# Feed-forward input products as seven block products of 320 columns instead of eight, with x parked in DRAM

## The chip, the cores and the metric

The kernel runs on one core of one Trainium2 chip. The metric is the device time of one execution in microseconds (us), the median of several runs. Engines are named as in the profile: PE (TensorE matmul), PEld (its weight load), DVE (VectorE), ACT (ScalarE), POOL (GpSimd), SP (the queue that issues most DMAs). PSUM is the memory that PE writes, SBUF the one that the other engines and the DMAs work in.

## The reference, cut to what matters

Two layers; in each a feed-forward half, a mixer and another feed-forward half. The change touches the feed-forward halves, which are this, on 640 tokens (512 latent, 128 context), D_MODEL = 1024 and D_FF = 2816:

```python
def swiglu(h, w_in, w_out):
    gate, up = jnp.split(h @ w_in, 2, axis=-1)
    return (jax.nn.silu(gate) * up) @ w_out

def adaln_sublayer(x, mod, s, g_pre, g_post, fn, weight):
    shift = mod[:, 3 * s, None]
    scale = mod[:, 3 * s + 1, None]
    gate = mod[:, 3 * s + 2, None]
    h = rmsnorm(x, g_pre) * (1 + scale) + shift
    y, aux = fn(h)
    return x + weight * gate * rmsnorm(y, g_post), aux
```

`mod` is SiLU(cond) @ mod_w[l] + mod_b[l], for two conditions (latent and context): 9 rows of 1024 per layer.

## The kernel before

**Arithmetic.** Every fp32 operand of a product is split into a rounded part `hi` and a rest `lo` (both fp32r), and a product is three passes: hi\*hi, hi\*lo, lo\*hi (`PASSES`). The split of a weight tile costs one ACT copy (line 102) and one DVE subtraction (line 103), of 128x1024 each.

**A feed-forward half (`ffn`).** The normed input lies transposed in `hT` (8 blocks of 128 features by 640 tokens, hi and lo). The 22 blocks of 128 hidden features, called f here, are worked in parts of 2, 4, 4, 4, 4, 4 (`PARTS`). For each f, `col_product` (line 467) forms the gate and the up product: 2 (gate, up) x 2 token groups (384 and 256 columns) x 8 feature blocks x 3 passes = 96 matmuls. `glu` (lines 512 and 513) makes silu(gate)\*up, and `split` (274, 275) gives `g`. After a part's f, `product` (line 573) multiplies `g` by the output weights, 120 matmuls of 512 columns for four f, and DVE adds the result to `yacc` (line 595). In the last part, tile after tile of 128 tokens is finished by `tail`: `emit` (products and the add of line 630), `post_norm` (399, 402), `pre_norm` (407), and `to_feature` (transposes 415, 418, 275) for the next sub-layer, in the order `TAIL_FFN`, where `m0` puts the products of the last f that were held back (`rest(1)`) between two tiles.

**Weights (`Stream`).** Tiles of 512 KB come in by SP (line 74) into three raw buffers, are split, and wait in five buffers of `whi` and `wlo` until `done`.

**Modulation rows (`mod_gen`).** Beside a feed-forward half DVE works out rows of `mod` for later sub-layers (lines 308 and 310: multiply-adds of 128x512), one unit at each `tick`. Of the 16 rows, the first half (called A; from 70 to 522 us) makes 7, the second (B; 901 to 1380 us) 3, the third (C; 1380 to 1864 us) 6, and the last (D; from 2204 us) none. Each half row ends in four small matmuls (line 332).

**Order.** Each engine runs its instructions in the order of its own queue; the framework fixes these orders when it builds the program. POOL has little to do here: the product with the gate in `post_norm` (399), small powers (391), and in A a chain of DMAs of its own for the bias tables (lines 1478 to 1490).

Of the kernel before, what the change touches and what calls it, by code (L numbers as in the profile page):

```python
# [44 lines left out]
TAIL_FFN = "e0 e1 p0 p1 e2 t0 p2 m0 e3 t1 p3 t2 e4 p4"  # L45
TAIL_MIX = "e0 e1 p0 p1 e2 t0 p2 e3 t1 p3 t2 e4 p4"
# [6 lines left out]


class Stream:
# [31 lines left out]
    def pump(self):
        while self.n_dma < min(len(self.specs), self.n_split + RAW_BUFS):
            self.load()
        while self._room():  # L90
            self.split()
            self.load()

    def split(self):
# [1824 lines left out]
```

## Time and profile before

| | us |
|---|---|
| median of 3 runs (2679.11 to 2680.49) | 2680.42 |
| the profiled execution: its own time | 2679.11 |
| the profiled execution: span from first to last instruction | 2677.3 |
| PE busy in that span | 2617.9 (98%) |
| DVE busy | 1535.6 (57%) |
| ACT busy | 929.4 (35%) |
| POOL busy | 218.9 (8%) |
| mean granted clock of TensorE | 0.995 of full speed |

The profiled execution took 1.8 us more than its span, and is 1.3 us below the median of the runs. The shares are means over stages: DVE's lies between 32% and 79% in single parts of the feed-forward halves. Busy time of PE counts matmuls whose ends are modelled; how fast it works is read from the time between the starts of matmuls of one kind.

### The profile page before, as it was taken

The numbers are of one execution on the slowest core, as the hardware profiler recorded it, in microseconds if no ns is written. First come the engines' busy times: TensorE is split into PE (matmuls) and PEld (weight loads), VectorE is DVE, ScalarE is ACT, GpSimd is POOL, SyncE is SP. The second block draws the span as 40 slices with busy tenths as digits, with TensorE's granted clock in tenths as the row PEclk, the third lists the DMA queues.
The fourth block names the chain that finished last, engine by engine and source line by source line (L and its number), as shares of the span: only waits on it lengthen the run. The fifth ranks groups of instructions, "written<-read, shape, count | busy, mean of one in ns | idle before, by whom it ended". The sixth has DMA issues, their size and how long they took to land.

```text
span 2677.3 us, 39659 instructions
## 1 busy us (share of the span) xinstructions
PE 2617.9 (98%) x16050; PEld 2353.1 (88%) x16050; DVE 1535.6 (57%) x2627; ACT 929.4 (35%) x1751; POOL 218.9 (8%) x284
## 2 busy tenths in 40 slices
PE   7999999999989999999999999999999999999998
PEld 6988999888766899999989889998999879999998
DVE  5877673655675755443377666535777764333334
ACT  4312222453465522222253222225555654222122
POOL 0000200301010000000020000003423200000001
PEclk9999999999989999999999999999999999999999
DMA  9665652222102444332236545322222223222221
GB/s 264 207 173 164 198 162 79 62 57 67 43 25 56 143 123 121 111 84 78 79 106 190 150 146 151 110 82 60 62 68 68 68 88 102 71 79 71 79 72 55
DMA packets 359719, 279.51 MB, mean 104 GB/s; under 512 B 43744, under 2 KB 296560, under 8 KB 359536
## 3 DMA queue, kind: packets, MB, share of 16 engines
q1 hardware_dynamic: 357232, 271.74, 35.0%
q0 software_dynamic: 1584, 3.93, 0.5%
q8 instruction: 126, 2.06, 0.3%
q10 hardware_dynamic: 720, 1.31, 0.1%
q14 instruction: 57, 0.47, 0.1%
HBM read 272.74 MB, written 8.11 MB: 105 GB/s over the span
## 4 chain that ended last, share of the span: by engine, by line
PE 61%; DVE 3%; DMA 2%; POOL 1%; issue 1%; ACT 1%; SPq 0%; DVEq 0%; POOLq 0%; ACTq 0%
PE ps L467 33%; PE ps L573 15%; PE ps L477 5%; PE ps L768 3%; DMA mraw<-in_mod_w_dram 1%; PE ps L1714 1%; PE ps L1695 1%; POOL tok L399 1%; PE sc L768 1%; PE ps L1665 1%; PE ps L1666 0%; DVE wlo L103 0%; DVE yacc L630 0%; DVE x L402 0%; PE ps L332 0%
## 5 line engine op out<-in xcount | busy, mean ns | idle before, releaser
L467 PE MATMUL ps<-hT,whi 128*128 128x384 f32 (+1 forms) x5760 | 1256.1, 309 | 6.7 <-DVE hT L275 3.6
L467 PEld LDWEIGHTS ps<-hT,whi 128*128 128x128 f32 x5760 | 968.1, 189 | 21.6 <-issue 7.8
L467 PE MATMUL ps<-hT,wlo 128*128 128x256 f32 (+1 forms) x2880 | 888.1, 308 | 0.0
L102 ACT CAST whi<-raw 128x1024 fp32r<-128x1024 f32 x312 | 327.4, 1051 | 968.6 <-PE ps L467 588.4
L103 DVE TENSOR_TENSOR wlo<-raw,whi 128x1024 fp32r<-128x1024 f32 x312 | 382.4, 1228 | 440.0 <-ACT whi L102 436.0
L467 PEld LDWEIGHTS ps<-hT,wlo 128*128 128x128 f32 x2880 | 545.5, 189 | 0.0
L573 PE MATMUL ps<-whi,g 128*128 128x512 f32 x1600 | 511.3, 395 | 4.2 <-ACT g L274 3.7
L573 PEld LDWEIGHTS ps<-whi,g 128*128 128x128 f32 x1600 | 300.3, 188 | 81.1 <-ACT g L274 5.0
L310 DVE SCALAR_TENSOR_TENSOR macc<-mraw,cc,macc 128x512 f32<-128x512 f32 x448 | 309.1, 747 | 34.7 <-DMA mraw<-in_mod_w_dram 34.5
L573 PE MATMUL ps<-wlo,g 128*128 128x512 f32 x800 | 317.5, 397 | 0.0
L477 PE MATMUL ps<-hT,whi 128*128 128x384 f32 (+1 forms) x1216 | 278.1, 316 | 0.0
L477 PEld LDWEIGHTS ps<-hT,whi 128*128 128x128 f32 x1216 | 204.1, 188 | 22.1 <-issue 15.3
L477 PE MATMUL ps<-hT,wlo 128*128 128x384 f32 (+1 forms) x608 | 188.9, 311 | 0.0
L573 PEld LDWEIGHTS ps<-wlo,g 128*128 128x128 f32 x800 | 150.2, 188 | 34.4
L399 POOL TENSOR_TENSOR tok<-yacc,G 128x1024 f32<-128x1024 f32 (+1 forms) x20 | 43.4, 2171 | 1538.2 <-DVE yacc L630 1535.5
L513 DVE TENSOR_TENSOR sg<-sg,ps 128x256 f32<-128x256 f32 (+1 forms) x176 | 85.1, 484 | 135.2 <-PE ps L467 129.3
L595 DVE TENSOR_TENSOR yacc<-yacc,ps 128x512 f32<-128x512 f32 x160 | 106.8, 685 | 89.7 <-PE ps L573 89.1
L512 ACT ACTIVATE sg<-ps 128x256 f32<-128x256 f32 (+1 forms) x176 | 76.3, 434 | 152.8 <-PE ps L467 101.2
L274 ACT CAST g<-sg 128x640 fp32r<-128x640 f32 (+2 forms) x96 | 65.6, 683 | 154.7 <-DVE sg L513 154.7
L477 PEld LDWEIGHTS ps<-hT,wlo 128*128 128x128 f32 x608 | 114.5, 188 | 1.1 <-issue 0.8
L275 DVE TENSOR_TENSOR g<-sg,g 128x640 fp32r<-128x640 f32 (+2 forms) x96 | 73.7, 768 | 52.5 <-ACT g L274 52.5
L1535 POOL TENSOR_TENSOR xn<-braw,mask 128x128 f32<-128x128 f32 x112 | 63.6, 597 | 136.0 <-DVE nb L1680 131.7
(358 smaller groups left out, 2374.4 us busy)
## 6 DMA issues: line engine op xcount, KB each, us to landing
raw<-in_ffn_w_in_dram SPq DMA_DIRECT2D x172, 512.0 KB
mraw<-in_mod_w_dram SPq DMA_DIRECT2D x128, 512.0 KB
raw<-in_ffn_w_out_dram SPq DMA_DIRECT2D x88, 512.0 KB
raw<-in_na_w_qkv_dram SPq DMA_DIRECT2D x24, 512.0 KB
raw<-in_ab_w_in_dram SPq DMA_DIRECT2D x22, 512.0 KB
raw<-in_mod_w_dram SPq DMA_DIRECT2D x32, 256.0 KB
G<-mod SPq DMA_DIRECT2D x12, 512.0 KB
mrow<-in_mod_b_dram SPq DMA_DIRECT2D x128, 32.0 KB
```

The costliest lines, as they stand in the source:

```text
L102: self.nc.scalar.copy(hi[:, :k * n], raw[:, :k * n])
L103: self.nc.vector.tensor_tensor(out=lo[:, :k * n], in0=raw[:, :k * n], in1=hi[:, :k * n].bitcast(F32), op=ALU.subtract)
L275: return a, nc.vector.tensor_tensor(out=lo, in0=src, in1=hi.bitcast(F32), op=ALU.subtract)
L310: nc.vector.scalar_tensor_tensor(out=acc[c], in0=raw[:, k2, :], scalar=w, in1=acc[c], op0=ALU.mult, op1=ALU.add)
L399: eng.tensor_tensor(out=yg[:, c0:c0 + n], in0=src, in1=G[cond_of(t)][:, c0:c0 + n], op=ALU.mult)
L467: nc.tensor.matmul(out=banks[grp], lhsT=w[a][:, k, :], rhs=hT[b][:, k, o:o + n], start=(k == 0 and (a, b) == (0, 0)), stop=(k == NK - 1 an ...
L477: nc.tensor.matmul(out=banks[grp], lhsT=w[a][:, k, :], rhs=hT[b][:, k, o:o + n], start=(k == 0 and (a, b) == (0, 0)), stop=(k == NK - 1 an ...
L512: nc.scalar.activation(out=sg[:, o:o + n], in_=banks[0][grp], func=AF.Silu)
L513: nc.vector.tensor_tensor(out=sg[:, o:o + n], in0=sg[:, o:o + n], in1=banks[1][grp], op=ALU.mult)
L573: nc.tensor.matmul(out=out, lhsT=g[a][kf][:, t * 128:(t + 1) * 128], rhs=w[b], start=(kf == 0 and (a, b) == (0, 0)), stop=(kf == len(fts) ...
L595: nc.vector.tensor_tensor(out=dst, in0=dst, in1=acc[t], op=ALU.add)
L768: nc.tensor.matmul(out=y[t][h], lhsT=hT[a][:, k, t * 128:(t + 1) * 128], rhs=ws[k // 2, h][b][:, k % 2, :], start=(k == 0 and (a, b) == (0 ...
```

## The change

Parts 1 to 5 of each feed-forward half (20 of 22 f, 80 in all) form [gate | up] by Strassen's scheme in Winograd's form. The block matrix of the weights has 2 x 2 blocks (feature halves by gate and up), that of the tokens too (feature halves by token halves of 320). Seven products `p1` to `p7` of 4 feature blocks x 3 passes = 12 matmuls of 320 columns each replace the 96 matmuls, so 84 for an f.

- **Weights.** A pair of raw tiles (gate G, up U) becomes four split tiles X, S, Z, V (S of half size). `_combine` makes their sums with four POOL operations of 128x512, in place in the raw buffers, once X has been split.
- **Tokens.** `combine` makes four sums of halves of `hT`, once in each half, in part 0 (two whole sums on POOL, two on DVE, four differences and four splits).
- **Results.** For each f ACT copies three results out of PSUM, DVE adds or multiplies four more from PSUM, and one more DVE product follows.
- **Space.** The sums of tokens take the room of x: x is written to DRAM by ACT's queue as it is made (`x_saved`) and read back by SP in the last part. `yacc` takes the x buffers.
- **Other.** `mod_gen` works in units of 256 KB (two DVE operations) instead of 512 KB (four); a tick between output products counts three times (`OUT_SHARE`); `load_gate` moves from part 2 to the last; `m0` falls away, instead the first output products of tile 0 run before the last two block products (`fill`); the loads of the first modulation rows come in pieces of 256 columns instead of 128; small tiles are padded to multiples of 64 bytes.

```diff
+    def _combine(self):
+        if not self.n_split:
+            return
+        _, _, kind, (g, *u) = self.specs[self.n_split - 1]
+        if kind != "X" or g in self.parts or u[0] not in self.raws:
+            return
+        G, U, S = self.raws[g], self.raws[u[0]], self.part_tile()
+        a, b = slice(0, 512), slice(512, 1024)
+        for out, in0, in1, op in (
+            (G[:, a], G[:, a], U[:, a], ALU.subtract), (S, U[:, b], G[:, a], ALU.subtract),
+            (U[:, a], U[:, a], U[:, b], ALU.add), (G[:, b], G[:, b], S, ALU.subtract),
+        ):
+            self.nc.gpsimd.tensor_tensor(out=out, in0=in0, in1=in1, op=op)
+        self.parts[g] = (S, self.n_pump)
...
+            def product(self, out, w, b, start):
+                for k in range(4):
+                    for a, c in PASSES:
+                        nc.tensor.matmul(
+                            out=out, lhsT=w[a][:, k, :], rhs=b[c][:, k, :], start=start and (k, a, c) == (0, 0, 0),
+                            stop=(k == 3 and (a, c) == PASSES[-1]), skip_group_check=not start,
+                        )
...
+            def p1(self):
...
+                self.X, self.Y = self.get("X"), bank([128, HALF])
+                self.product(self.Y, self.half(self.X, 0), B[0, 0], True)
+                nc.scalar.copy(self.t[:, 0], self.Y)
...
+            def p2(self):
+                W, t = bank([128, HALF]), self.t
+                self.product(W, self.half(self.X, 1), B[1, 0], True)
+                nc.vector.tensor_tensor(out=t[:, 0], in0=t[:, 0], in1=W, op=ALU.add)
+                nc.scalar.activation(out=t[:, 0], in_=t[:, 0], func=AF.Silu)
+                self.done("X")
...
+            def p6(self):
+                self.product(self.Y, self.get("S"), C[2], False)
+                nc.scalar.copy(self.t[:, 1], self.Y)
+                self.done("S")
...
+            def p5(self):
+                self.wz, self.Z = self.get("Z"), bank([128, HALF])
+                self.product(self.Z, self.half(self.wz, 0), C[1], True)
...
+            def p7(self):
+                self.V, t = self.get("V"), self.t
+                self.product(self.Y, self.half(self.V, 0), C[3], False)
+                nc.scalar.copy(t[:, 2], self.Y)
+                nc.vector.tensor_tensor(out=t[:, 2], in0=t[:, 2], in1=self.Z, op=ALU.add)
...
+            def p4(self):
+                t = self.t
+                self.product(self.Y, self.half(self.wz, 1), C[4], False)
+                nc.vector.tensor_tensor(out=t[:, 0], in0=t[:, 0], in1=self.Y, op=ALU.mult)
...
+            def p3(self):
+                t = self.t
+                self.product(self.Z, self.half(self.V, 1), B[1, 1], False)
+                nc.vector.tensor_tensor(out=t[:, 1], in0=t[:, 1], in1=self.Z, op=ALU.add)
+                nc.scalar.activation(out=t[:, 1], in_=t[:, 1], func=AF.Silu)
+                nc.vector.tensor_tensor(out=t[:, 1], in0=t[:, 1], in1=t[:, 2], op=ALU.mult)
+                self.out(1 if self.last else 0, 2)
+                self.done("V")
...
+            us = [Unit(f, g, i, f == fts[-1]) for i, f in enumerate(fts)]
+            for i, u in enumerate(us):
+                todo = [] if i else [u.p1]
+                todo += [u.p2] + ([us[i - 1].p3] if i else []) + [u.p6, u.p5, u.p7]
+                todo += [us[i + 1].p1, u.p4] if i + 1 < len(us) else [fill, u.p4, u.p3]
...
-        N, NQ = 512, 4
+        N, NQ = 512, NK
...
-TAIL_FFN = "e0 e1 p0 p1 e2 t0 p2 m0 e3 t1 p3 t2 e4 p4"
+TAIL = "e0 e1 p0 p1 e2 t0 p2 e3 t1 p3 t2 e4 p4"
```

How instructions move on DVE, in the units of a part of half A. `raw` and `whi`, `wlo` are weights and their parts, `sg` and `g` the hidden features before, `xn`, `tok` (f by turns) and `g` those now, `G` the tile of S, `macc` and `mraw` the modulation rows. Before, one f and the beginning of the next:

```order
L513 TENSOR_TENSOR sg<-sg,ps 128x384
L310 SCALAR_TENSOR_TENSOR macc<-mraw,cc,macc 128x512 x4
L103 TENSOR_TENSOR wlo<-raw,whi 128x1024
L513 TENSOR_TENSOR sg<-sg,ps 128x256
L310 SCALAR_TENSOR_TENSOR macc<-mraw,cc,macc 128x512 x2
L275 TENSOR_TENSOR g_1_1655<-sg,g_1_1651 128x640
L310 SCALAR_TENSOR_TENSOR macc<-mraw,cc,macc 128x512 x5
L103 TENSOR_TENSOR wlo<-raw,whi 128x1024
```

And now, the same place:

```order
L671 TENSOR_TENSOR xn<-xn,ps 128x320
L384 SCALAR_TENSOR_TENSOR macc<-mraw,cc,macc 128x512
L157 TENSOR_TENSOR wlo<-raw,whi 128x1024
L701 TENSOR_TENSOR tok<-tok,ps 128x320
L384 SCALAR_TENSOR_TENSOR macc<-mraw,cc,macc 128x512
L703 TENSOR_TENSOR tok<-tok 128x320
L384 SCALAR_TENSOR_TENSOR macc<-mraw,cc,macc 128x512
L157 TENSOR_TENSOR wlo<-G_2042,whi 128x512
L350 TENSOR_TENSOR g_1_1755<-tok,g_1_1751 128x640
L157 TENSOR_TENSOR wlo<-raw,whi 128x1024
L384 SCALAR_TENSOR_TENSOR macc<-mraw,cc,macc 128x512
L688 TENSOR_TENSOR xn<-xn,ps 128x320
```

An f had two weight splits, two products with PSUM and one split of `g` on DVE; it has four weight splits (one of half size), four operations with PSUM, one product in SBUF and the split of `g`, with the multiply-adds of the modulation rows between them.

On POOL, in half A around the DMAs of the bias tables (lines 1478 to 1490 before, 1689 to 1701 now). Before:

```order
L391 TENSOR_TENSOR r<-r,nhalf 128x1 x5
L1478 DMA rpb_flat<-tok 16x1x2
L1479 DMA rpb_flat<-tok 16x1x2
L1485 DMA rpb_rows<-rpb_flat 240x48 x16
L1490 DMA rel<-rpb_rows 16x16x384 x8
L399 TENSOR_TENSOR tok<-yacc_716,G_2218 128x1024
```

And now:

```order
L142 TENSOR_TENSOR raw<-raw,G_2868 128x512
L1689 DMA rpb_flat<-tok 16x1x2
L1690 DMA rpb_flat<-tok 16x1x2
L1696 DMA rpb_rows<-rpb_flat 240x48 x16
L1701 DMA rel<-rpb_rows 16x16x384
L142 TENSOR_TENSOR raw<-raw 128x512
L1701 DMA rel<-rpb_rows 16x16x384
L142 TENSOR_TENSOR G_3153<-raw 128x512
```

POOL, idle in the parts before, now makes four sums for each f, and one f's sums stand behind the waits of the bias tables' DMAs.

## Rows read from the trace of the kernel before

**Rows 1.** The page: busy time by engine, and the chain that ended last.

```profile
PE 2617.9 (98%) x16050; PEld 2353.1 (88%) x16050; DVE 1535.6 (57%) x2627; ACT 929.4 (35%) x1751; POOL 218.9 (8%) x284
PE 61%; DVE 3%; DMA 2%; POOL 1%; issue 1%; ACT 1%; SPq 0%; DVEq 0%; POOLq 0%; ACTq 0%
```

**Rows 2.** Busy time by stretch: parts 1 and 4 of A, one of B, C, D.

```profile
core 0: us, PE busy (x) PEld busy (x) DVE busy (x) ACT busy (x) POOL busy (x), PEclk, DMA share, GB/s
84.00:171.00 87.00, 87.00 (x535) 79.34 (x536) 68.84 (x101) 19.41 (x27) 0.00 (x0) 1.00 0.61 183
...
345.00:431.00 86.00, 86.00 (x533) 78.75 (x526) 50.20 (x75) 18.37 (x24) 0.00 (x0) 1.00 0.44 124
947.80:1032.70 84.90, 84.90 (x513) 78.89 (x512) 37.25 (x50) 19.21 (x26) 0.00 (x0) 1.00 0.35 102
1428.00:1514.00 86.00, 86.00 (x526) 79.15 (x520) 59.37 (x87) 18.78 (x25) 0.00 (x0) 1.00 0.55 158
2248.50:2332.70 84.20, 84.20 (x505) 78.74 (x504) 27.09 (x33) 19.21 (x26) 0.00 (x0) 1.00 0.23 69
```

**Rows 3.** The same view, line 467 alone, in a part's input products of D.

```profile
2248.50:2304.70 56.20, 56.18 (x384) 56.17 (x383) 1.00 0.25 76
```

**Rows 4.** Timeline of PE in D (start, us, engine, line): matmuls of 384 and 256 columns.

```profile
2249.05 0.51 PE L467 MATMUL ps<-hT,whi 128*128 128x384 f32 x2
...
2249.57 0.51 PE L467 MATMUL ps<-hT,whi 128*128 128x384 f32 x2
...
2253.04 0.40 PE L467 MATMUL ps<-hT,whi 128*128 128x256 f32 x2
...
2253.40 0.40 PE L467 MATMUL ps<-hT,whi 128*128 128x256 f32 x2
```

**Rows 5.** DVE's groups by form (count, busy us, mean ns, idle before and its releaser).

```profile
L103 DVE TENSOR_TENSOR wlo<-raw,whi 128x1024 fp32r<-128x1024 f32 x312 | 382.4, 1228 | 440.0 <-ACT whi L102 436.0 <-ACT wlo L906 1.2 <-issue 0.7
L310 DVE SCALAR_TENSOR_TENSOR macc<-mraw,cc,macc 128x512 f32<-128x512 f32 x448 | 309.1, 747 | 34.7 <-DMA mraw<-in_mod_w_dram 34.5
L595 DVE TENSOR_TENSOR yacc<-yacc,ps 128x512 f32<-128x512 f32 x160 | 106.8, 685 | 89.7 <-PE ps L573 89.1
L275 DVE TENSOR_TENSOR g<-sg,g 128x640 fp32r<-128x640 f32 x80 | 65.9, 823 | 44.1 <-ACT g L274 44.1
L513 DVE TENSOR_TENSOR sg<-sg,ps 128x384 f32<-128x384 f32 x88 | 48.7, 553 | 130.9 <-PE ps L467 129.3 <-ACT sg L512 1.5
L513 DVE TENSOR_TENSOR sg<-sg,ps 128x256 f32<-128x256 f32 x88 | 36.5, 414 | 4.4 <-ACT sg L512 4.4
L308 DVE TENSOR_SCALAR macc<-mraw,cc 128x512 f32<-128x512 f32 x64 | 29.8, 480 | 3.8 <-DMA mraw<-in_mod_w_dram 3.6
```

**Rows 6.** POOL's groups by form.

```profile
L399 POOL TENSOR_TENSOR tok<-yacc,G 128x1024 f32<-128x1024 f32 x15 | 37.0, 2463 | 1093.6 <-DVE yacc L630 1093.6
L1423 POOL TENSOR_TENSOR wlo<-ident,sums 128x512 f32<-128x512 f32 x8 | 8.3, 1040 | 70.5 <-DVE sums L1421 36.0 <-ACT hT L274 15.0 <-DVE nb L1337 13.8
L399 POOL TENSOR_TENSOR tok<-yacc,G 128x512 f32<-128x512 f32 x5 | 6.5, 1294 | 444.6 <-DVE yacc L630 441.9 <-DMA out_dram<-x 2.7
```

**Rows 7.** Timeline of DVE and POOL after half A: two splits beside POOL.

```profile
523.09 3.50 DVE L275 TENSOR_TENSOR hT<-xn,hT 128x512 fp32r<-128x512 f32 x2
523.32 2.72 POOL L399 TENSOR_TENSOR tok<-yacc,G 128x1024 f32<-128x1024 f32 x1 [2.13 <-DVE yacc L630]
```

**Rows 8.** Timelines of PE and of DVE in the tail of half A.

```profile
499.96 1.09 PE L415 MATMUL ps<-ident,xn 128*128 128x128 f32 x8 [0.71 <-DVE xn L407]
...
506.60 1.29 DVE L275 TENSOR_TENSOR hT<-xn,hT 128x512 fp32r<-128x512 f32 x2
...
510.60 0.75 DVE L407 TENSOR_SCALAR xn<-x,r 128x1024 f32<-128x1024 f32 x1 [0.44 <-POOL r L391]
```

**Rows 9.** Timeline of POOL in half A: the first and the last of the bias DMAs.

```profile
280.61 0.54 POOL L1478 DMA_DIRECT2D rpb_flat<-tok  x1 [256.27 <-DVE tok L1475]
...
299.02 4.48 POOL L1490 DMA_DIRECT2D rel<-rpb_rows  x8 [3.19 <-DMA rpb_rows<-rpb_flat]
```

More of the change, by code (lines that the diff above doesn't have):

```diff
@@ L74, in load, with _loads @@
             self.nc.sync.dma_start(out=view[p0:p0 + np_, :, c0:c0 + src.shape[-1]], in_=src)
-        self.raws.append(raw)
+        self.raws[self.n_dma] = raw
         self.n_dma += 1
+    def _loads(self):
+        while self.n_dma < len(self.loads) and self.n_dma - self.freed < RAW_BUFS:
+            self.load()
     def _room(self):
@@ L99, in split @@
         else:
+            self.held.add(key)
             hi = self.w_pool.tile([128, 1024], F32R, tag="whi", name="whi", bufs=W_BUFS)
@@ L113, in get, with done @@
         self.n_get += 1
+        self.got.append(key)
         return self.ready.pop(0)
-    def done(self, n=1):
-        self.n_done += n
+    def done(self, n=1, key=None):
+        for _ in range(n):
+            k = self.got.pop(0 if key is None else self.got.index(key))
+            self.held.discard(k)
         self.pump()
@@ L429, in to_feature, with tail @@
         return ins
-    def tail(emit, pieces, G, nxt, m, mid=None, between=None):
+    def tail(emit, pieces, G, nxt, m, junk, dst=None, between=None):
         xn = {}
@@ L436, in step @@
             emit(t)
-            post_norm(t, pieces(t), G, last=nxt is None)
+            post_norm(t, pieces(t), G, junk, dst and dst[t], last=nxt is None)
         def pre(t):
@@ new lines, in products @@
+                def products():
+                    for h in range(2):
+                        ws = [stream.get(("out", l, j, f, h)) for f in fts[::2]]
+                        for tiles in ((0, 1, 2), (3, 4)):
+                            acc = {t: bank() for t in tiles}
+                            for kf in range(len(fts)):
+                                for t in tiles:
+                                    product(acc[t], t, kf, [w[:, kf % 2, :] for w in ws[kf // 2]])
+                                if tiles[-1] == NT - 1 and kf % 2 == 1:
+                                    stream.done()
+                                if kf < len(fts) - 1:
+                                    yield
+                            for t in tiles:
+                                dst = yacc[t][:, h * 512:(h + 1) * 512]
+                                if p == 0:
+                                    nc.scalar.copy(dst, acc[t])
+                                else:
+                                    nc.vector.tensor_tensor(out=dst, in0=dst, in1=acc[t], op=ALU.add)
+                            yield
@@ L632, in pieces @@
-                def pieces(t):
-                    if nxt is None:
-                        return [(yacc[t][:, h * 512:(h + 1) * 512], h * 512, 512) for h in range(2)]
-                    return [(yacc[t], 0, D)]
-                return tail(emit, pieces, G, nxt, m, lambda: rest(1))
+                prep += combine()
+            else:
+                strassen(fts, g, fill)
+            if p == 3 and first:
+                spread_bias(g[0][0])
+            if not last:
+                for _ in todo:
+                    stream.pump()
+                    tick(OUT_SHARE)
@@ L640, in start, with pieces @@
+        reload((4,), ("b40",))
+        def pieces(t):
+            if nxt is None:
+                return [(yacc[t][:, h * 512:(h + 1) * 512], h * 512, 512) for h in range(2)]
+            return [(yacc[t], 0, D)]
+        junk = fp.tile([128, D], BF16, tag="mraw", name="mraw", bufs=2)
+        return tail(emit, pieces, G, nxt, m, junk, yacc)
     def start(sp, l, s):
@@ L787, in finish_with @@
             G = gate()
-            return tail(emit, lambda t: [(y[t][h], 512 * h, 512) for h in range(2)], G, nxt, m, between=between)
+            junk = wo.tile([128, D], BF16, name="junk", bufs=1)
+            return tail(emit, lambda t: [(y[t][h], 512 * h, 512) for h in range(2)], G, nxt, m, junk, between=between)
         return products, finish_with
```

379 lines of the change are left out of this document (221 added, 158 removed).

## The prediction

> **What bounds the kernel now.** I read the page first: PE is busy 98% of the span, the other engines 57% and less [rows 1], and 61% of the chain that ended last is PE's. So whatever PE is spared, the kernel is spared, as long as nothing else takes over. What could take over shows only part by part, so next came the busy times by stretch [rows 2]. The reader should look at two columns there. PE is busy without a gap in every part, at a granted clock of 1.00, so a part lasts as long as its matmuls: 84.2 us in D, 84.9 in B, 86.0 in C, 87.0 falling to 86.0 in A (four parts). DVE in the same parts is busy 27.1, 37.3, 59.4 and 68.8 to 50.2 us. The difference is the modulation rows, of which D makes none and A seven. POOL is idle. Then I read what one matmul costs [rows 3, 4], what DVE's and POOL's operations cost [rows 5, 6], and what happens when both want SBUF [rows 7].
>
> **PE: what is removed.** Three matmuls of 384 columns start every 0.52 us, three of 256 every 0.36 us [rows 4], so 0.173 and 0.120 us each. No stretch of before has steady products of 320 columns; 320 is midway, so I take 0.1463, which is also the mean over the 384 matmuls of a part (56.2 us / 384 [rows 3]). The bounds are 0.120 and 0.173. A part of four f goes from 384 matmuls to 336, 56.2 to 49.2 us: 7.0 us less. Twenty such parts: **-140 us** if PE never waits. The 120 matmuls of 512 columns of a part stay.
>
> **DVE: what is added.** I build the demand of a part without modulation rows from durations [rows 5]. One f has three splits of 1.23 us and one of half size, 0.69 (between 0.82 at 640 and 0.55 at 384 columns), four operations with PSUM and one in SBUF at 0.48 (between 0.41 and 0.55), and the split of g, 0.82: together 7.6 us. Four f are 30.4, the four output weights 4.9 and ten adds to yacc 6.9, so 42 us where 27 to 29 stood. The modulation rows take 309 + 30 us and, with the short add behind the four small matmuls, some 352 for 16 rows, 22 each. The new ticks give parts 1 to 4 each (28 + 48) of 328 shares, 23%. That is 36 us a part in A (7 rows), 31 in C (6), 15 in B (3). DVE's demand of a part becomes **78 (A), 73 (C), 57 (B), 42 (D)**. PE's new part time is the old less 7: 80, 79, 78, 77. DVE alone would still just fit.
>
> **POOL: what is added, and the port.** An f has four sums of 128x512 on POOL. The nearest rows are 1.29 us (same shape, same three kinds of operand) and 1.04 (same shape) [rows 6]; I take 1.28, so 16 sums are 20.5 us a part, on an idle engine. But they are not beside DVE's work. At 523 us DVE makes two splits of 128x512 that take 1.29 us elsewhere [rows 8]; while a POOL product of 2.4 us runs they take 3.50 together, and POOL's product 2.72 [rows 7]: each waited for the other. So a POOL sum keeps DVE from operations with two SBUF operands, and the reverse. The page SBUF — State Buffer of the Trainium skill (SBUF: two separate sides) says that GpSimd and a DVE operation with two SBUF inputs hold a shared pair of ports exclusively, for a whole instruction, and that the other fully blocks. By that rule, the trace agrees: 3.50 us where 1.29 was free. Taking it or leaving it out is worth 20 us a part.
>
> What can run beside a POOL sum is DVE's work with PSUM: 16 x 0.48 + 6.9, about 15 us a part, 16 in A. So the two engines need, together, between (perfect overlap) 82, 78, 62 and 47 us and (none) 98, 94, 78 and 63 us in A, C, B and D. With PE at 80, 79, 78 and 77:
> - **D**: PE still sets the part, 77 plus 0.5 for handovers. 4 x -6.5 = **-26**.
> - **B**: at most 78, equal to PE; I take 79 against 84.9. 4 x -6 = **-24**.
> - **C**: 79 to 94; the middle of the demand, 86, against 86.0. **0** (bounds -28 and +32).
> - **A**: 82 to 98; the middle, 90.5, against 86.7 on average. 4 x 3.8 = **+15** (bounds -19 and +47).
> I take the middle because DVE's queue is in order: a POOL sum meets PSUM work only by chance, but DVE also waits at times (34.7 us for modulation weights [rows 5]), when POOL is free to run.
>
> **Part 5 and the tail.** No modulation rows run there, so its units give -7. But `m0` is gone. After tile 0's transposes PE did 48 held-back matmuls of 256 columns (5.8 us), the products of tile 3 (24 of 512 columns at 28.0/120 us, 5.6) and tile 1's transposes (1.1). Tile 2's normed x is ready only at 510.60 + 0.75 us [rows 8]. Without the 5.8 us PE gets to tile 2's transposes at 501.05 + 5.6 + 1.1 = 507.7, and waits 3.7 us. In A, B, C that leaves -3.3 each; D has no transposes, -7: **-17**.
>
> **Part 0.** The sums of tokens are ten DVE operations of 1280 columns (1.54 us, scaled from 1.23) and two on POOL (3.1, from 2.46): 21 us that take turns. In B, C and D the products of the second token group and the output products, some 25 us, lie beside them; I charge 2 us each. In A only 14 us of output products do, with modulation rows among them: 8 (0 to 20). **+14**.
>
> **Costed at nothing.** Writing x out (15 tiles) and reading it back (20) moves 18 MB, through DMA engines that are busy a quarter to two thirds of the time [rows 2]; uncovered, a late x would stall one tile's `post_norm` by the time of one 512 KB load, two to three us. POOL's bias DMAs last 23 us, from 280.6 to 303.5 [rows 9], and one f's sums stand behind them; they come in a part's output phase, 28 us, before that f is needed. ACT has 19 us in a part [rows 2] and gets 1.5 casts and three copies more for each f: even at the 1.23 us of a DVE split 22 us, and half of the part stays free. The first modulation loads change their pieces, not their bytes: 0, between -4 and +4.
>
> **The sum.** -26 - 24 + 0 + 15 - 17 + 14 = -38 us, on an execution of 2679.1 (span 2677.3 and 1.8 around it): **2641 us**. The median of the runs lies 1.3 above that execution, which is less than the 0.2% (5.4 us) that can be told from no change.
>
> **Rivals.**
> 1. *The port costs little and PE stays the bound everywhere.* The POOL sums fall into DVE's PSUM work and its waits. For it: DVE was idle 20% and more of even the fullest part. Then A and C also give -7 a part, part 0 costs nothing: -28 x 4 - 17, **2550 us**. Chance 0.22.
> 2. *Slower: DVE and POOL take turns in A and C with no overlap, and PE starves there.* Parts of 98 and 94 us, part 0 at +25, the tail at -10, B and D at -42: +47 + 32 + 25 - 10 - 42 = +52, **2731 us**. It decides once the parts of A and C are on average over 6 us longer than before, about 93 and 92. For it: the in-order queue, and loads of modulation weights that now come in halves, two buffers deep. Against it: no part before left DVE less than 18 us idle. It is the rule of the SBUF page at its full price. Chance 0.18.
> 3. *No change: the raw buffers are a loop.* The next up tile is loaded only when V of this f is split; then come the load (512 KB at the 300 GB/s that 69 GB/s at a share of 0.23 mean [rows 2], 1.8 us and a latency), four sums (5.1) and the splits of S, Z, V (about 4): 12 us, as long as an f's 12.3 on PE. If each sum also waits for one DVE split (1.23), it is 17, and 5 us a part are left after the buffers' slack, in B and D too: 2641 + 40, **2681 us**. Chance 0.12.
> 4. *The seventh is not saved:* matmuls of 320 columns cost like those of 384, 0.173. A part's units take 58.1 us instead of 56.2: **2720 us** or so. Against it: the cost follows the columns [rows 4]. Chance 0.04.
>
> **How the numbers follow.** The forecast has 0.44. Faster by over 0.2%: 0.44 + 0.22 and a third of rival 3, 0.70; within 0.2%: 0.08; slower: 0.22. The range takes in the middle of A's and C's bounds on both sides and leaves out the far ends of rivals 1 and 2: 2585 to 2710.
>
> **What would show it.** Right: block products in D start every 0.146 us and its parts last 77 to 78 us; in A the parts last about 90 with DVE busy for nearly all of it, PE's idle time ending on DVE's splits of weights; POOL's sums take 1.3 us alone and over 2 us next to a split. Wrong: parts of A at 80 us (rival 1); parts over 93 (rival 2); gaps of PE in D that end on a split behind a load or a POOL sum (rival 3); 0.17 us for 320 columns (rival 4).

## The result and the profile after

| | before | after |
|---|---|---|
| median, us | 2679.77 (2677.99 to 2680.49, 4 runs) | 2819.40 (2815.01 to 2820.90, 4 runs) |
| span of the profiled execution, us | 2677.3 | 2813.1 |
| mean granted clock of TensorE | 0.995 | 0.965 |

The ratio is 1.052 (95% interval 1.0505 to 1.0531): the change makes the kernel 5% slower, where the forecast said 1.5% faster. The page, busy time and chain, beside [rows 1]:

```profile
PE 2557.8 (91%) x15090; PEld 2257.3 (80%) x15090; DVE 2051.6 (73%) x3079; ACT 1176.1 (42%) x2179; POOL 723.6 (26%) x612
PE 33%; DVE 15%; DMA 6%; POOL 5%; issue 4%; ACT 4%; SPq 0%; DVEq 0%; ACTq 0%; POOLq 0%
```

PE has 960 matmuls less, and they cost what was forecast: in D three matmuls of 320 columns start every 0.44 us, so 0.1467 each (the timeline of PE after; start, us, engine, line):

```profile
2478.75 0.46 PE L647 MATMUL ps<-hT,whi 128*128 128x320 f32 x2
2479.19 0.46 PE L647 MATMUL ps<-hT,whi 128*128 128x320 f32 x2
```

But PE's share of the chain fell from 61% to 33%. Busy time by stretch of the kernel after, one row per part (the first and the last of A, one of B, C, D), columns as in [rows 2]:

```profile
93.50:197.30 103.80, 88.31 (x490) 75.22 (x488) 96.57 (x118) 33.59 (x50) 29.92 (x19) 0.94 0.47 136
393.00:512.40 119.40, 84.76 (x490) 74.92 (x489) 90.11 (x121) 29.97 (x45) 23.22 (x16) 0.86 0.47 125
1123.00:1208.80 85.80, 80.51 (x466) 73.50 (x465) 66.57 (x81) 30.16 (x45) 24.24 (x16) 0.98 0.40 113
1625.50:1721.50 96.00, 86.64 (x482) 76.38 (x481) 83.30 (x105) 29.84 (x45) 25.07 (x16) 0.93 0.46 131
2478.30:2560.00 81.70, 77.87 (x457) 71.82 (x456) 45.56 (x56) 30.13 (x45) 22.16 (x16) 1.00 0.26 78
```

PE now has gaps in every part, in D too, where DVE is busy for only 45.6 of 81.7 us, and the granted clock falls below 1.00 where the gaps are large. Where the 135.8 us of span went is read from the starts of PE's products at the border of each stage (lengths in us; the last two columns are runs of the experiments below):

| stage | before | after | e2 | e9 |
|---|---|---|---|---|
| start to part 1 of A | 84.1 | 93.5 | 88.4 | 85.4 |
| part 0 of B, C, D | 47.2, 48.4, 44.1 | 53.3, 57.9, 52.5 | 49.2, 54.3, 46.8 | 44.6, 52.3, 45.3 |
| parts 1 to 4 of A | 347.7 | 418.9 | 372.2 | 344.3 |
| parts 1 to 4 of B | 341.6 | 345.8 | 313.1 | 319.4 |
| parts 1 to 4 of C | 345.5 | 382.2 | 329.4 | 318.4 |
| parts 1 to 4 of D | 337.1 | 327.4 | 310.0 | 311.4 |
| part 5 and tail, A to D | 90.3, 90.3, 90.3, 91.8 | 92.5, 91.8, 92.4, 89.6 | 89.1, 87.4, 90.5, 84.8 | 90.5, 88.3, 87.8, 84.8 |
| the two mixers | 378.4, 340.4 | 376.4, 338.9 | 376.4, 339.2 | 376.4, 341.0 |

The largest items are the parts of A (+71) and C (+37) and the four part 0 (+33 with the start). DVE's and POOL's groups by form in the kernel after (count, busy us, mean ns, idle before and its releaser) show who is slow:

```profile
L157 DVE TENSOR_TENSOR wlo<-raw,whi 128x1024 fp32r<-128x1024 f32 x400 | 500.1, 1253 | 103.8 <-ACT whi L156 95.7 <-issue 0.7 <-PE ps L1201 0.7
L384 DVE SCALAR_TENSOR_TENSOR macc<-mraw,cc,macc 128x512 f32<-128x512 f32 x448 | 402.7, 931 | 71.7 <-DMA mraw<-in_mod_w_dram 70.9 <-DVE xn L688 0.3
L761 DVE TENSOR_TENSOR x<-x,ps 128x512 f32<-128x512 f32 x160 | 105.4, 682 | 36.8 <-PE ps L736 36.4
L157 DVE TENSOR_TENSOR wlo<-G,whi 128x512 fp32r<-128x512 f32 x72 | 84.4, 1173 | 71.8 <-ACT whi L156 71.1
L142 POOL TENSOR_TENSOR raw<-raw 128x512 f32<-128x512 f32 x160 | 223.4, 1396 | 1256.9 <-DVE wlo L157 1191.1 <-issue 41.5 <-DMA mraw<-in_mod_w_dram 24.3
L142 POOL TENSOR_TENSOR raw<-raw,G 128x512 f32<-128x512 f32 x72 | 120.0, 1666 | 0.0
L619 POOL TENSOR_TENSOR tok<-hT,hT 128x1280 f32<-128x1280 f32 x8 | 34.7, 4333 | 27.6 <-DVE g L350 27.6
```

The adds from PSUM (line 761) cost what they did, 0.682 us against 0.685 [rows 5]. The multiply-adds, which read two tiles of SBUF, went from 0.747 to 0.931 us, and the split of an S tile, the one that comes with the sums, takes 1.17 us for half a tile, hardly less than the 1.25 of a whole one. The timeline of DVE and POOL during one f of A shows why:

```profile
132.85 1.30 POOL L142 TENSOR_TENSOR raw<-raw 128x512 f32<-128x512 f32 x1 [8.41 <-DVE wlo L157]
133.09 1.60 DVE L384 SCALAR_TENSOR_TENSOR macc<-mraw,cc,macc 128x512 f32<-128x512 f32 x1
134.22 1.61 POOL L142 TENSOR_TENSOR G<-raw 128x512 f32<-128x512 f32 x1
134.61 1.57 DVE L703 TENSOR_TENSOR tok<-tok 128x320 f32<-128x320 f32 x1
135.80 1.54 POOL L142 TENSOR_TENSOR raw<-raw 128x512 f32<-128x512 f32 x1
136.11 1.79 DVE L384 SCALAR_TENSOR_TENSOR macc<-mraw,cc,macc 128x512 f32<-128x512 f32 x1
137.30 1.74 POOL L142 TENSOR_TENSOR raw<-raw,G 128x512 f32<-128x512 f32 x1
137.82 1.77 DVE L157 TENSOR_TENSOR wlo<-G,whi 128x512 fp32r<-128x512 f32 x1
```

They take turns. Each DVE row ends 0.35 to 0.56 us after the POOL row that began just before it, and each later POOL row takes 1.5 to 1.7 us where the first took 1.30. Four DVE operations fill the 6.5 us from 133.09 to 139.59; without POOL two such multiply-adds take 0.76 each, the product in SBUF 0.49 and the split 0.69 (e2, below). Back to back the eight would take 7.9 us (four times 1.30, and 2.7); from 132.85 to 139.59 they took 6.7, so the turns still overlap a little.

The two longest items of what PE waits for in the kernel after (us in total, times, longest):

```profile
PE ps L647 <- ACT xn L677: 56.7, 33, 3.3
PE ps L647 <- ACT tok L677: 33.5, 21, 5.4
```

Line 677 is ACT's copy of `p6`'s product out of PSUM, which `p7` needs before it may go on in the same bank. In parts 1 to 4 of D these are PE's only waits. The timeline of one of them (POOL, ACT, PE):

```profile
2483.57 1.30 POOL L142 TENSOR_TENSOR raw<-raw 128x512 f32<-128x512 f32 x1
2483.64 0.62 ACT L156 CAST whi<-G 128x512 fp32r<-128x512 f32 x1 [2.94 <-PE ps L647]
2484.90 1.05 ACT L156 CAST whi<-raw 128x1024 fp32r<-128x1024 f32 x1 [0.26 <-POOL raw L142]
2485.86 0.42 ACT L677 COPY xn<-ps 128x320 f32<-128x320 f32 x1
2486.32 0.42 PE L647 MATMUL ps<-b,whi 128*128 128x320 f32 x1 [0.82 <-ACT xn L677]
```

The copy is a small operation, but on ACT's queue it stands behind the cast of the Z tile, which waits for POOL's third sum; so a sum of weights that nobody needs yet holds up PE.

The longest single wait of PE, 22.4 us, is of another kind. It lies in part 4 of A, behind a wait of 8.6 us at the same place (timelines of PE and SP):

```profile
418.33 0.64 PE L647 MATMUL ps<-b,whi 128*128 128x320 f32 x1 [8.60 <-ACT whi L156]
441.67 0.64 PE L647 MATMUL ps<-b,wlo 128*128 128x320 f32 x1 [22.43 <-DVE wlo L157]
420.04 21.33 SPq L369 DMA_DIRECT2D mraw<-in_mod_w_dram  x11
```

Between the split of `g` at 417.80 and the split of an S tile at 440.93 DVE makes 22 multiply-adds of modulation rows and nothing else, at the pace of their 11 loads. In its queue they stand ahead of a split that PE waits for.

Such gaps cost more than their length. The granted clock was 1.00 up to 412.8 us and fell while PE stood in the wait of 8.6 us; behind the long wait it is still at the lower of its two levels (1.2 of 2.4 GHz), as the view by stretch shows:

```profile
442.10:446.90 4.80, 4.80 (x19) 4.80 (x19) 2.92 (x3) 0.43 (x1) 0.02 (x1) 0.50 0.71 212
```

In this stretch three matmuls of 320 columns start every 0.80 us, from 447.35 us on again every 0.44. So part of what the gaps cost shows as longer busy time of PE.

### The profile page after: what moved, and what is told of

The parts are those of the page before. It is cut to its first block, busy times and chain, and to the rows that moved or that the text cites. A ratio compares the mean times of both kernels' runs of the same rounds, so it can differ in the third digit from the quotient of the medians.

```text
span 2813.1 us, 39476 instructions
## 1 busy us (share of the span) xinstructions
PE 2557.8 (91%) x15090; PEld 2257.3 (80%) x15090; DVE 2051.6 (73%) x3079; ACT 1176.1 (42%) x2179; POOL 723.6 (26%) x612
## 4 chain that ended last, share of the span: by engine, by line
PE 33%; DVE 15%; DMA 6%; POOL 5%; issue 4%; ACT 4%; SPq 0%; DVEq 0%; ACTq 0%; POOLq 0%
PE ps L647 12%; PE ps L736 10%; DVE wlo L157 5%; PE ps L560 5%; DVE macc L384 4%; DMA mraw<-in_mod_w_dram 3%; POOL raw L142 2%; ACT whi L156 2%; PE ps L978 2%; POOL G L142 1%; DMA raw<-in_ffn_w_in_dram 1%; PE ps L550 1%; DMA raw<-in_ffn_w_out_dram 1%; DVE g L350 1%; PE ps L1925 1%
## 5 line engine op out<-in xcount | busy, mean ns | idle before, releaser
L647 PE MATMUL ps<-hT,whi 128*128 128x320 f32 x2560 | 576.2, 313 | 2.0 <-DVE xn L688 1.9
L647 PE MATMUL ps<-b,whi 128*128 128x320 f32 x1920 | 448.2, 320 | 112.3 <-ACT xn L677 56.7
L142 POOL TENSOR_TENSOR raw<-raw 128x512 f32<-128x512 f32 x160 | 223.4, 1396 | 1256.9 <-DVE wlo L157 1191.1
L647 PEld LDWEIGHTS ps<-hT,whi 128*128 128x128 f32 x2560 | 436.9, 192 | 8.0 <-DVE xn L688 2.6
L647 PEld LDWEIGHTS ps<-b,whi 128*128 128x128 f32 x1920 | 330.1, 194 | 134.7 <-ACT xn L677 65.7
L647 PE MATMUL ps<-hT,wlo 128*128 128x320 f32 x1280 | 399.6, 312 | 0.0
L647 PE MATMUL ps<-b,wlo 128*128 128x320 f32 x960 | 303.6, 316 | 22.4 <-DVE wlo L157 22.4
L560 PE MATMUL ps<-hT,whi 128*128 128x384 f32 (+1 forms) x1216 | 277.6, 316 | 0.1
L647 PEld LDWEIGHTS ps<-hT,wlo 128*128 128x128 f32 x1280 | 244.6, 191 | 0.4 <-issue 0.4
L560 PEld LDWEIGHTS ps<-hT,whi 128*128 128x128 f32 x1216 | 203.9, 188 | 21.9 <-issue 15.2
L647 PEld LDWEIGHTS ps<-b,wlo 128*128 128x128 f32 x960 | 186.8, 195 | 22.8 <-DVE wlo L157 22.8
L156 ACT CAST whi<-G 128x512 fp32r<-128x512 f32 x72 | 44.6, 620 | 254.1 <-POOL G L142 118.7
L550 PE MATMUL ps<-hT,whi 128*128 128x384 f32 (+1 forms) x640 | 140.9, 311 | 4.8 <-DVE hT L350 4.8
```

The source lines that it names most:

```text
L142: self.nc.gpsimd.tensor_tensor(out=out, in0=in0, in1=in1, op=op)
L156: self.nc.scalar.copy(hi[:, :k * n], raw[:, :k * n])
L550: nc.tensor.matmul(out=banks[grp], lhsT=w[a][:, k, :], rhs=hT[b][:, k, o:o + n], start=(k == 0 and (a, b) == (0, 0)), stop=(k == NK - 1 an ...
L560: nc.tensor.matmul(out=banks[grp], lhsT=w[a][:, k, :], rhs=hT[b][:, k, o:o + n], start=(k == 0 and (a, b) == (0, 0)), stop=(k == NK - 1 an ...
L647: nc.tensor.matmul(out=out, lhsT=w[a][:, k, :], rhs=b[c][:, k, :], start=start and (k, a, c) == (0, 0, 0), stop=(k == 3 and (a, c) == PASS ...
```

## The experiments

Three theories. **A**, taking turns: DVE and POOL exclude each other at SBUF (rival 2 of the prediction). **B**, order: PE waits for things that are cheap but stand in a queue behind something that waits for a POOL sum. **C**, load: DVE simply has too much to do in A and C.

| run | what | median, us | ratio to before (95%) |
|---|---|---|---|
| e1 | bias DMAs behind A's tail | 2803.40 | 1.0464 (1.0445 to 1.0483) |
| e2 | sums of weights on DVE | 2636.74 | 0.9838 (0.9820 to 0.9856) |
| e3 | no sums of weights | 2623.81 | 0.9787 (0.9772 to 0.9801) |
| e4 | an eighth of the multiply-adds | 2680.01 | 0.9997 (0.9987 to 1.0006) |
| e5 | e3, and POOL makes sums nobody reads | 2831.89 | 1.0570 (1.0548 to 1.0592) |
| e6 | copy of `p6` on DVE | 2792.86 | 1.0426 (1.0410 to 1.0441) |
| e7 | e2, token sums on DVE too | 2622.56 | 0.9786 (0.9772 to 0.9801) |
| e8 | e2, modulation rows spread | 2603.34 | 0.9719 (0.9703 to 0.9735) |
| e9 | e7 and e8 | 2590.12 | 0.9665 (0.9650 to 0.9679) |
| e10 | e9, OUT_SHARE 2 | 2592.85 | 0.9679 (0.9664 to 0.9693) |
| e11 | e9, OUT_SHARE 1 | 2598.55 | 0.9694 (0.9680 to 0.9709) |
| e12 | kernel before, rows spread | 2688.48 | 1.0037 (1.0023 to 1.0051) |

**e1, the bias DMAs.**

```diff
-            if p == 3 and first:
-                spread_bias(g[0][0])
...
-        return tail(emit, pieces, G, nxt, m, junk, yacc)
+        done = tail(emit, pieces, G, nxt, m, junk, yacc)
+        if first:
+            spread_bias(g[0][0])
+        return done
```

> The 26 DMAs of the bias tables are moved from behind part 3 of half A to behind its tail; nothing else. Theory B (the order): with them on POOL, the framework plans the sums of weights late and lets 22 multiply-adds of modulation rows pass the split of an S tile on DVE's queue; PE waits 31 us for it near 410 to 441 us. Then part 4 of A falls from 119 to about 100 us and the whole to about 2797 us. Rival (DVE is simply too full, the multiply-adds would be paid for elsewhere): A gets no shorter, 2815 to 2820 us.

16.0 us less than the change (2803.40 against 2819.40). Part 4 of A went from 119.4 to 100.6 us; parts 1 to 4 of A by stretch:

```profile
93.50:485.20 391.70, 339.19 (x1931) 296.74 (x1929) 357.11 (x457) 123.42 (x185) 99.14 (x64) 0.96 0.51 143
```

The run of 22 multiply-adds is gone from DVE's queue, and parts 1 to 4 of A are 391.7 us instead of 418.9. The DMAs cost 6.7 us in the mixer instead (383.1 against 376.4), so the whole gains less than A. So the order of DVE's queue was upset by DMAs on POOL's. It is 16 of 140 us, not the cause.

**e2, the sums of weights on DVE.**

```diff
-            self.nc.gpsimd.tensor_tensor(out=out, in0=in0, in1=in1, op=op)
+            self.nc.vector.tensor_tensor(out=out, in0=in0, in1=in1, op=op)
```

> The four sums of weights of each f run on DVE in place of POOL. Theory A (DVE and POOL take turns at SBUF): a POOL sum of 1.3 us becomes a DVE operation of about 0.6, nothing excludes anything; a part of A has 78 + 10 us of DVE work and lasts about 90 instead of 105, of C about 86 instead of 96: about 2690 us. Theory C (DVE's load alone is the bound): A and C get longer by up to the 10 us a part that DVE is given more, B and D stay: 2820 to 2880 us. Theory B (PE waits for copies that stand on ACT's queue behind casts which wait for sums): the gaps of 4.3 us in each part of D, which end on ACT's copy, shrink to 2 or less, D's parts from 81.8 to about 79.5.

One word changed, and the kernel is 183 us faster than with the change as it came, and 1.6% faster than before. It did better than any theory said. Busy time of e2, and one part each of A, B, D by stretch:

```profile
PE 2505.9 (95%) x15090; PEld 2224.8 (85%) x15090; DVE 2036.3 (77%) x3399; ACT 1175.9 (45%) x2179; POOL 257.4 (10%) x292
184.80:269.90 85.10, 81.05 (x477) 72.88 (x474) 74.60 (x116) 30.16 (x45) 0.00 (x0) 0.99 0.52 149
1053.10:1131.00 77.90, 77.90 (x465) 71.98 (x465) 64.43 (x97) 30.35 (x45) 0.00 (x0) 1.00 0.43 124
2314.00:2391.30 77.30, 77.30 (x457) 71.80 (x456) 49.65 (x72) 30.10 (x45) 0.00 (x0) 1.00 0.27 82
```

B and D have no gap left, at 77.9 and 77.3 us. The reader should compare DVE's busy time: 2036.3 us with 320 more operations, 2051.6 without them. DVE's groups by form tell where the time came from:

```profile
L384 DVE SCALAR_TENSOR_TENSOR macc<-mraw,cc,macc 128x512 f32<-128x512 f32 x448 | 321.9, 758 | 36.9 <-DMA mraw<-in_mod_w_dram 36.7
L142 DVE TENSOR_TENSOR raw<-raw 128x512 f32<-128x512 f32 x160 | 109.6, 685 | 0.2
L157 DVE TENSOR_TENSOR wlo<-G,whi 128x512 fp32r<-128x512 f32 x72 | 49.4, 686 | 16.0 <-ACT whi L156 16.0
```

A sum takes 0.69 to 0.76 us on DVE; the 320 take 225 us (109.6 in this row; 54.8, 49.4 and 11.0 in four smaller groups). The multiply-adds are back at 0.758 us, the split of S at 0.686. Theory C alone is out: with more work on DVE, A and C became 47 and 53 us shorter.

**e3, no sums.** As the change, with `_combine` making no sums (S is read from the up tile's first half).

> The sums of weights are left out (the splits read the raw tiles as they are, so the products are not the reference's). Theories A and B together: nobody takes turns and no cast waits for a sum, DVE's 78 us a part are under PE's 80; parts of A 82, C 80, B 79, D 77.5 us, the whole about 2620 us. Theory C (DVE's load alone): A and C stay at 95 us and more, about 2730 us. D at 77.5 instead of 81.8 would be theory B's part of it.

2623.81, as theories A and B said, though not in A: its parts last 88.6 us on average where 82 were expected, so something in A costs time without POOL's sums too. D's parts 2 to 4 are 77.5 us; one of them by stretch:

```profile
2382.10:2459.70 77.60, 77.60 (x458) 71.86 (x457) 40.83 (x56) 30.39 (x45) 0.00 (x0) 1.00 0.27 82
```

Against e3, e2's sums on DVE cost 13 us; the changed kernel's on POOL cost 196.

**e4, an eighth of the multiply-adds.**

```diff
-        N, NQ = 512, NK
+        N, NQ = 512, 1
...
-                pending = ffn(fp, l, s, pending, (mod_gen(fp, todo), 16 * len(todo) + 4) if todo else None, nxt, banks0)
+                pending = ffn(fp, l, s, pending, (mod_gen(fp, todo), 2 * len(todo) + 4) if todo else None, nxt, banks0)
```

> The modulation rows are summed over 128 of 1024 features instead of all (7 of 8 multiply-adds and their loads are left out, so the rows are not the reference's). All theories in which DVE is too full in A and C (alone or by turns with POOL): the parts of A, B and C become like those of D, 82 us: about 2655 us. If the multiply-adds are not what makes A and C long (order of sums and copies alone): parts of A and C stay over 90 us, the whole over 2740 us.

2680.01, 25 us above what was expected, and 139 us below the change: the parts of A, B and C average 86.6, 83.3 and 84.5 us, those of D keep their 81.7 after the first. So the sums on POOL are dear where DVE has the multiply-adds to do; but 4 us a part stay lost in D, where there are none.

**e5, turns without the wait.** e3, and for each f four sums on POOL that nobody reads:

```diff
+        junk = self.part_tile()
+        for _ in range(4):
+            self.nc.gpsimd.tensor_tensor(out=junk, in0=U[:, a], in1=U[:, b], op=ALU.add)
```

> As e3 (sums of weights left out, so the products are not the reference's), but POOL makes four sums of 128x512 for each f into a tile that nobody reads: the sharing of SBUF is there, the wait for a sum is not. Theory A (turns): DVE's operations with two SBUF operands get longer again (multiply-adds 0.93 us on average instead of 0.76, splits of S over 1 instead of 0.69), the parts of A and C are 10 to 15 us longer than in e3, about 2720 us; D stays at 77.5 us, where DVE has room. Theory B (the wait alone): as e3, 2620 to 2635 us, all durations of DVE as in e3.

No operation reads these sums (only the load of the gate in the last part waits for their tile), and they cost 208 us over e3: the run is as slow as the change. It is more than expected, because B and D lose too (parts 1 to 4 of A, B, C, D: 420.4, 349.4, 377.8, 342.7 us, against 354.5, 315.8, 333.0, 313.7 in e3). The groups by form of e3:

```profile
L152 DVE TENSOR_TENSOR wlo<-raw,whi 128x1024 fp32r<-128x1024 f32 x400 | 495.9, 1242 | 127.6 <-ACT whi L151 119.4 <-issue 0.7 <-PE ps L1196 0.7
L379 DVE SCALAR_TENSOR_TENSOR macc<-mraw,cc,macc 128x512 f32<-128x512 f32 x448 | 326.8, 763 | 78.3 <-DMA mraw<-in_mod_w_dram 77.9
```

and of e5, with POOL's:

```profile
L155 DVE TENSOR_TENSOR wlo<-raw,whi 128x1024 fp32r<-128x1024 f32 x400 | 573.8, 1437 | 104.6 <-ACT whi L154 99.4 <-issue 0.7 <-PE ps L1199 0.7
L382 DVE SCALAR_TENSOR_TENSOR macc<-mraw,cc,macc 128x512 f32<-128x512 f32 x448 | 368.9, 855 | 70.1 <-DMA mraw<-in_mod_w_dram 69.9
L140 POOL TENSOR_TENSOR G<-raw 128x512 f32<-128x512 f32 x288 | 473.8, 1646 | 1076.7 <-DMA raw<-in_ffn_w_in_dram 1060.4
```

DVE's busy time is 199 us more than in e3 (2049.6 against 1850.6) for the same 3079 instructions. Taking turns alone is enough for the whole loss. One reservation: the sums of e5 run in a burst when the up tile lands, those of the change when X is split, so the places differ. Parts 1 to 4 of D show it: they lose 29 us to e3 here and 14 with the change. One of PE's waits there, 2.5 us at 2504.84, ends on the copy of `p6` behind ACT's cast of `g`, which waits for a DVE product that takes 1.55 us beside a POOL sum instead of 0.49. A turn that DVE alone could afford reaches PE by way of a queue.

**e6, the copy of `p6` on DVE.**

```diff
-                nc.scalar.copy(self.t[:, 1], self.Y)
+                nc.vector.tensor_copy(self.t[:, 1], self.Y)
```

> The changed kernel with its sums on POOL; only the copy of p6's product out of PSUM goes to DVE instead of ACT. Theory B (the copy stands on ACT's queue behind a cast that waits for a POOL sum): the gaps of 0.8 to 1.5 us before p7 go, D's parts fall from 81.7 to 78 or 79, B's from 86 to 83, about 50 us in all if A and C follow by 3 each: 2765 us. Rival (PE's gaps in D come from the sharing of SBUF): D stays at 81.7 and the gaps end on DVE now: 2820 us.

2792.86, 26.5 us less than the change, half of what was expected. The sums stay on POOL. D's part falls to 77.7 us, where e2 and e3 have 77.3 and 77.5, and the waits in D to almost nothing; one part of D by stretch, and all of PE's waits in D's parts 1 to 4:

```profile
2472.00:2549.70 77.70, 77.34 (x458) 71.81 (x457) 47.29 (x60) 28.74 (x41) 22.25 (x16) 1.00 0.27 82
PE ps L647 <- DVE xn L677: 2.1, 4, 1.0
```

B falls from 86.5 to 84.5 a part, where e2 has 78.3; A and C rise by 2.8 and 0.5, as DVE got more to do there. So theory B is shown in D: the loss there is the copy's place on ACT's queue. For A and C this run does not separate place from load, because PE now waits for the same copy on DVE's queue, which is fuller. PE's longest item in parts 1 to 4 of C in e6:

```profile
PE ps L647 <- DVE xn L677: 29.4, 8, 6.3
```

**e7, the token sums on DVE.** As e2, and `whole_of` uses `nc.vector` for all four sums.

> As e2 (sums of weights on DVE), and the two token sums of POOL in part 0 go to DVE too, so that POOL has none of the new work. If taking turns costs in part 0 as well (4.3 us for each of POOL's two, against about 1.6 on DVE): 2 to 4 us less in each of the four part 0, 2625 us. If part 0 is bound by DVE's own work: no change or up to 3 us more each, 2636 to 2650.

14.2 us less than e2. The start to part 1 of A is 84.2 us and part 0 of D 43.9 (before: 84.1 and 44.1). A token sum takes 1.49 us on DVE where it took 4.33 on POOL. All four part 0 and the start are 225.2 us (B 45.1, C 52.0), against 223.8 before, 238.7 in e2 and 257.2 with the change: on DVE the token sums cost next to nothing. In the profiled executions the parts of A give 5.7 us of this back (377.9 against 372.2).

**e8, the rows spread.** As e2, with a table of rows in place of the rule (layer, row):

```diff
-            todo = [] if i else [(l, 3 * s + 2)]
...
+            todo = FFN_ROWS[l, s]
...
+    (0, 0): [(0, 2), (0, 3), (0, 4), (0, 5), (0, 6), (0, 7)],
+    (0, 2): [(0, 8), (1, 0), (1, 1), (1, 3), (1, 4)],
+    (1, 0): [(1, 2), (1, 5), (1, 6), (1, 7)],
+    (1, 2): [(1, 8)],
```

> As e2, and the modulation rows are spread otherwise: A makes 6 of 16 instead of 7, B 5 instead of 3, C 4 instead of 6, D 1 instead of 0, each row still before its use. If in e2 A and C are bound by DVE's work (a row is some 22 us, 5.5 of each part): A falls by 5 to 6 us a part, C from 82 to 79, B and D stay, as DVE has 13 and 27 us of room there: about 2600 us. If not (PE waits on the order of the small matmuls behind the rows): 2630 us or more.

2603.34, 33 us less than e2: A's parts 1 to 4 went from 372.2 to 341.8, C's from 329.4 to 318.4, B's from 313.1 to 321.0, D's by 1.

**e9, both.**

> e7 and e8 together: sums of weights and of tokens on DVE, modulation rows 6, 5, 4 and 1. If the two gains are independent (14 us from part 0 in e7, 33 us from the parts of A and C in e8): about 2590 us. If part 0 of A, where the rows run too, gives it back: 2600 us.

2590.12, the best version: 3.4% faster than before. A part each of A, B, D by stretch:

```profile
170.50:253.60 83.10, 80.85 (x475) 72.12 (x474) 79.13 (x123) 30.87 (x46) 0.00 (x0) 1.00 0.54 155
1020.10:1099.60 79.50, 79.50 (x482) 71.94 (x480) 72.74 (x112) 30.35 (x45) 0.00 (x0) 1.00 0.51 149
2271.20:2348.60 77.40, 77.40 (x458) 71.86 (x457) 49.72 (x72) 30.09 (x45) 0.00 (x0) 1.00 0.27 82
```

PE is busy without a gap again in these parts of B and D. A still has gaps, and DVE is busy there for 79 of 83 us.

**e10 and e11, OUT_SHARE 2 and 1.** As e9, with the one number changed.

> As e9, with OUT_SHARE 2 instead of 3: fewer multiply-adds between the output products and more between the block products. If PE's waits in A (for ACT's g and for sums of rows) come from a backlog of DVE in the output phases: A 3 to 4 us a part shorter, 2575 to 2580 us. If DVE's total in A is what counts: within 5 us of e9.

> As e9, with OUT_SHARE 1. By the backlog theory: like e10 or better, 2570 to 2580 us; if the multiply-adds then stand ahead of the operations with PSUM in the block products: slower than e9, 2600 us or more.

Neither helps: e10 is 2.7 us slower than e9, less than the intervals can tell apart, and e11 8.4. How the multiply-adds are shared out within a part matters little; their number in a half does (e8).

**e12, the kernel before with the rows spread.** The table of e8 in the kernel before, with `load_gate` moved to the last part.

> The kernel before with the modulation rows spread as in e8 (and the gate loaded in the last part, after its row). If the gain of e8 and e9 is the seven products' and the rows only make room for them: PE is busy throughout before, so within 5 us of 2680. If spreading the rows gains by itself: 2660 us or less.

2688.48, 10 us slower than the kernel before on the same chip and not within 5 of 2680. The trace spreads them over the start (2.0), the parts of A (2.9) and B (3.1) and part 0 of D (3.4), and the cause stays open. For e9 it settles one question: spreading the rows gains nothing by itself, and against e12 the seven products gain 98 us.

Not tried: the sums on ACT, and more raw or weight buffers.

## Why the prediction was wrong

By terms, the change of span in us (forecast, measured from the stage table, and with the sums on DVE):

| term | forecast | measured | e2 |
|---|---|---|---|
| parts of D | -26 | -10 | -27 |
| parts of B | -24 | +4 | -29 |
| parts of C | 0 | +37 | -16 |
| parts of A | +15 | +71 | +25 |
| part 5 and tail | -17 | +4 | -11 |
| part 0 | +14 | +33 | +15 |
| mixers | 0 | -3 | -3 |
| sum | -38 | +136 | -46 |

- **PE's saving was right.** 0.1467 us for 320 columns against 0.1463 forecast, and rival 4 is out. Without POOL's sums D's part is 77.3 to 77.5 us, the forecast's 77.5; DVE's load of 42 us in D is 40.8 in e3.
- **The step that failed: "I take the middle because DVE's queue is in order: a POOL sum meets PSUM work only by chance, but DVE also waits at times".** POOL's sums did not run in DVE's waits, and the waits came on top. Counted over the trace, the 64 sums in parts 1 to 4 of C take 100.5 us, of which 93.5 lie beside DVE operations with two SBUF operands, 7.6 beside ones with PSUM and 0.8 beside an idle DVE; in A it is 81.3, 7.3 and 10.2 of 97.7. The queue in order puts the next operation on SBUF behind one with PSUM at once, and from then on the two engines alternate (the timeline at 132.85). Parts 1 to 4 by stretch, C with the change, then A and C of e3, which has no sums (A without the stall of the bias DMAs is the row of e1):

```profile
1530.20:1912.30 382.10, 341.76 (x1921) 302.10 (x1920) 336.02 (x418) 121.52 (x183) 99.22 (x64) 0.95 0.46 133
87.40:441.90 354.50, 330.76 (x1937) 292.94 (x1935) 307.69 (x463) 124.04 (x185) 14.82 (x26) 0.97 0.60 173
1414.30:1747.30 333.00, 322.16 (x1922) 289.79 (x1921) 276.24 (x419) 120.82 (x183) 0.00 (x0) 0.99 0.53 151
```

  DVE's longest wait in the same stretch of A in e1, and of C with the change (us in total, times, longest):

```profile
DVE macc L384 <- DMA mraw<-in_mod_w_dram: 25.9, 26, 2.8
DVE macc L384 <- DMA mraw<-in_mod_w_dram: 27.1, 18, 5.1
```

  DVE is busy for 89.3 us a part in A (e1) and 84.0 in C: the sums added 12.4 and 15.0 to the 76.9 and 69.1 of e3. So much the middles of 90.5 and 86 had right. But the parts last 97.9 and 95.6: DVE is idle for 8.7 and 11.5 us of each, over half of it waiting for loads of modulation weights, the wait that the forecast put at nothing as time for POOL. PE's clock adds its share: in C its matmuls keep it busy for 341.8 us at a granted clock of 0.95, in e3 for 322.2 at 0.99. That the lengths come out at the bounds without overlap, 98 and 94 (rival 2), is therefore partly luck. How much of them is the turns and how much the waits stays open: no run takes the waits away, and in C of e3, where DVE is idle for 57 us, PE has only 11 us without work.
- **B and D were costed as if an engine with spare time could not hold PE up.** "PE still sets the part, 77 plus 0.5 for handovers" was 77 plus 4.7 in D. DVE and POOL together need 63 us there without overlap and PE 77, and yet PE waits, since what counts is one copy on ACT's queue behind a cast behind a POOL sum (e6). In B that copy is PE's main wait too, but e6 gives back only 2 of the 8 us a part. Rival 3 had the size (5 us a part, in B and D too) and the culprit, a POOL sum, but the wrong queue: the raw buffers are not the bound, as e6 leaves them as they are and removes the gaps in D.
- **Part 0** was forecast at +14 from two POOL sums of 3.1 us a half; they take 4.33. Of the +33 measured, 18.5 go when the sums of weights leave POOL (e2) and 13.5 more when the token sums do (e7); what DVE's operations then cost is 1.4.
- **Part 5 and the tail.** -17 was right about D without the waits (-7.0 in e2, as forecast). In A, B and C the wait for a normed x, forecast at 3.7 us, is 5.4 to 5.9 with the change, and the same handovers as in D's parts (3.8 us a half) eat the rest.
- **The bias DMAs, "costed at nothing".** The reason given was that an f's sums are needed 28 us later. They cost 16 us (e1), by a way that was not looked for: queues are ordered when the program is built, and 22 multiply-adds came to stand ahead of a split that PE waits for.
- **Writing x out and reading it back**: no DMA of x ends a wait of PE, as forecast.
- **Rival 2** was priced at 2731, with parts of 98 and 94 us, near those measured, but with B and D at -42 and the tail at -10, where they came to -6 and +4. The Trainium skill's page SBUF — State Buffer (SBUF: two separate sides) says that the shared ports are held for a whole instruction and the other engine fully blocks. The runs agree that one waits for the other: a split takes 1.44 us in e5 and 1.24 in e3. Its full price, 1.30 us of DVE's time for each sum or 20.8 us a part, is not what they show: 15.0 in C and 12.4 in A.

That the sum of e2 comes out near the forecast is partly chance: C is better and A worse than the forecast had them.

## What to carry to other kernels

An idle engine is not free capacity when it takes turns with a busy one. Before work goes to POOL, add to DVE's time what the turns cost it (for operations with two SBUF operands), and compare that with DVE's own duration for the same work. Here a POOL sum of 1.3 us cost DVE as much as the 0.7 us that the sum takes on DVE, and the right choice was worth 183 us of 2819. And an engine's spare time says nothing about an operation's place in its queue: look at what stands ahead of each small copy that PE waits for.

## What was not expected of the hardware

A sum on POOL takes as much of DVE's time as the same sum on DVE. With no sums of weights DVE is busy for 1850.6 us (e3), with the 320 sums on DVE for 2036.3 (e2), and with the 320 on POOL for 2051.6. So each POOL sum stretched DVE's records by 0.63 us on average (201 / 320), while one on DVE adds 0.58 (186 / 320; its own record is 0.70, and neighbouring records overlap a little). Using POOL saved DVE nothing.
